# A masked prefix sum read at one row: the two blind blocks as the first pair of the buffer cycle, and two remainders a round

## The chip, the cores and the metric

The kernel runs on one core of a Trainium2 chip. The metric is the time of one execution on the device in microseconds. The profile is of one such execution; its times count from the start of its span. "Landing" is the moment at which a transfer's last part has signalled. TensorE does the matmuls, VectorE the small vector work, ScalarE (ACT) and SyncE (SP) issue the loads, and GpSimd (POOL) writes a few constants.

## The reference

```python
B, S, D = 8, 8192, 512            # x [B, S, D] f32, lengths [B] int64, w [D, D] f32
mask = (pos < lengths[:, None, None]).astype(np.float32)
cs = np.cumsum(x * mask, axis=1)
midpoints = (lengths // 2).clip(0)
mid_features = cs[b_idx, midpoints, :]
out = np.matmul(mid_features[:, None, :], w).squeeze(1)
```

Only one row of the prefix sum is wanted for each batch, so out[b] is the sum of the first min(lengths[b] // 2 + 1, lengths[b]) rows of x[b], times w. How many rows that is, the kernel learns when it has read `lengths`.

## The kernel before

**Blocks and rests.** The rows of a batch are read in blocks of 512 rows (1 MB, `P` = 128 partitions x `G` = 4 rows). What is left over, under 512 rows, is the batch's rest. It is read in pieces of 256, 128, 64, 32 or 16 rows into one of three buffers `rem`. Everything is summed by TensorE into one accumulator `s_ps`: the weights (`cur`, `cur_rem`) are 0 or 1 and say to which of the eight batches a block belongs or, for a rest, which partitions count. A block is four matmuls (one for each of its four rows a partition) that run in four column groups of the array.

**The blind blocks.** The first block of batch 0 and that of batch 1 are loaded before `lengths` is known (L187 to L190), into a tile of their own, `first`. Their weights `cur_first` are 1 where the batch has such a block. They are multiplied ahead of the loop (L549 to L552).

**The cycle.** All other whole blocks, but for the last one of the last batch, go in pairs through a buffer `xt` of `NS` = 3 places, `PER` = 6 blocks a round. VectorE works out from `lengths` how many there are (`addr[1]`), at which row each begins (`addr`), and the weights of each (`since`). Four engines run over the same rounds with semaphores between them:

- SP (L216 to L247): `load(k)` waits until place k is free (`s_free[k]`), issues one 2 MB load, or two of 1 MB where the two blocks do not touch, or a single block at the end, then loads the next two addresses.
- TensorE (L555 to L574): in place k it first issues `BUSY[k]` idle matmuls (`keep_busy`), which keep the array busy while it waits, then waits for `s_full[k]`, multiplies the pair, and then the rest that this round has for place k.
- VectorE (L471 to L494): when TensorE is done with place k it writes the weights of that place's next pair into `cur[:, k]`, which frees the place for SP; in the same way `cur_rem[:, k]` for rests, which frees a rest buffer for ACT.
- ACT (L275 to L324): issues the loads of the rests, three a round, so eight rests take three rounds.

A test ahead of each place (`pairs`, L153) skips it where no block is left for it, on each of these engines. A rest is multiplied in a round as long as `some`, which falls by three a round, says so.

**The end.** The last whole block of the last batch has its own tile `last`, loaded in four parts on SP's queue behind all others (L253 to L255). TensorE adds its first two quarters to `s_ps`, then signals VectorE (`tell`, L530), which copies `s_ps` to `s_sb` in two halves. TensorE folds and turns these into `t_ps`, VectorE moves them to `t_sb`, and 16 matmuls with w give the output, which goes out in two halves.

**VectorE's list.** VectorE begins with 59 steps in a fixed order, and others wait on their count: `DVE_ADDR` (15) lets SP start, `DVE_FIRST` (32) lets TensorE multiply the blind blocks, `DVE_MASK` (49) lets it enter the loop, `DVE_ALL` (59) ends the list.

Of the kernel before, what the change touches and what calls it, by code (L numbers as in the profile page):

```python
# [12 lines left out]
ds = bass.ds  # L13
# [4 lines left out]
def kernel(  # L18
# [34 lines left out]
    PER = 2 * NS  # L53
    ROUNDS = -(-(B * S // 2 // BLK - BLIND - 1) // PER)
    ITEMS = BLIND + ROUNDS * PER
    KC = D // P
# [8 lines left out]
    WT = G * B  # L65
    RR = -(-B // NS)
    xf = x.rearrange("b s d -> (b s) d")
# [14 lines left out]

    first = sb("first", [P, BLIND, G, D])
    xt = sb("xt", [P, NS, 2, G, D])
    last = sb("last", [P, G, D])
    rem = sb("rem", [P, NS, G, D])
    wt = sb("wt", [P, KC, D])
    lens1 = sb("lens1", [1, 2 * NS * RR], I32)
    len_f = sb("len_f", [1, B])
# [26 lines left out]
    row_last = sb("row_last", [1, 1], I32)  # L116
    cur_first = sb("cur_first", [P, BLIND, B])
    cur = sb("cur", [P, NS, 2, B])
# [7 lines left out]
    thr = sb("thr", [P, G], I32)  # L126
    table = sb("table", [P, max(B * (WT + 1), NS * RR * WT)])
    cur_rem = sb("cur_rem", [P, NS, WT])
    fold_i = sb("fold_i", [P, B], I32)
# [12 lines left out]
    s_done, s_free, s_full = [[sem(f"{n}{k}") for k in range(NS)] for n in ("done", "free", "full")]  # L142
    s_rdone, s_rfree, s_rem = [[sem(f"{n}{q}") for q in range(NS)] for n in ("rdone", "rfree", "rem")]
    s_last = [sem(f"last{h}") for h in range(len(ENDS))]
    s_first = [sem(f"first{b}") for b in range(BLIND)]
    s_w, s_len1, s_out = sem("w"), sem("len1"), sem("out")
# [33 lines left out]

    nc.sync.dma_start(out=lens1[:, :2 * B], in_=lens_words).then_inc(s_len1, 16)

# [4 lines left out]
    for b in range(BLIND):  # L187
        nc.sync.dma_start(
            out=first[:, b], in_=xf[b * S:b * S + BLK].rearrange("(p g) d -> p g d", g=G)
        ).then_inc(s_first[b], 16)  # L190

# [17 lines left out]
    def _(sp):  # L209
# [5 lines left out]

        def load(k):  # L216
            take(sp, s_free[k], 1)

            def block(h, n=1):

                to = xt[:, k].rearrange("p h g d -> p (h g) d")[:, h * G:(h + n) * G]
                sp.dma_start(
                    out=to, in_=xf[ds(sp.snap(at[h]), n * BLK)].rearrange("(p g) d -> p g d", g=n * G)
                ).then_inc(s_full[k], 16)

            sp.reg_alu(apart, at[1], at[0], ALU.subtract)
            with sp.If_cmp(left, 2 * k + 2, "IS_GE"):
                with sp.If_cmp(apart, BLK, "IS_EQ"):
                    block(0, 2)
                    sp.sem_inc(s_full[k], 16)  # L230
                with sp.Else():
                    block(0)
                    block(1)
            with sp.Else():
                block(0)
                sp.sem_inc(s_full[k], 16)
            if k == NS - 1:
                sp.wait_ge(s_dve, DVE_ALL)
            sp.load(at, addr[:, ds(sp.snap(off, min_val=BLIND + 2, max_val=ITEMS - 2), 2)])
            sp.reg_alu(off, off, 2, ALU.add)  # L240
            sp.reg_alu(off, off, ITEMS - 2, ALU.min)
# [19 lines left out]
    def _(act):  # L261
        hint = act.mark_branch_hint_location()
        alu = act.reg_alu
        base, at, t = [act.alloc_register(f"act_{n}") for n in ("base", "at", "t")]
        words = [act.alloc_register(f"act_n{i}") for i in range(2 * NS)]
        pair, top = act.alloc_register("act_pair"), 2 * NS * (RR - 1)
        some = act.alloc_register("act_some")
        act.reg_mov(base, 0)
        act.reg_mov(pair, 0)
        act.reg_mov(some, B)  # L270
        act.memzero(lens1[:, 2 * B:])  # L271
        for q in range(NS):
            act.memzero(rem[:, q]).then_inc(s_rfree[q], 1)  # L273
        act.wait_ge(s_len1, 16)
        with act.Fori(0, RR):  # L275
            act.load(words, lens1[:, ds(act.snap(pair, min_val=0, max_val=top), 2 * NS)])
            def rest(q):
# [37 lines left out]
                alu(base, base, S, ALU.add)  # L315
            for q in range(NS):
                if q < B - NS * (RR - 1):
                    rest(q)
                else:
                    with act.If_cmp(some, q + 1, "IS_GE"):  # L320
                        rest(q)
            less(act, some, NS)
            alu(pair, pair, 2 * NS, ALU.add)
            alu(pair, pair, top, ALU.min)  # L324
# [10 lines left out]
    def _(pool):  # L335
# [8 lines left out]
        pool.iota(fold_i[:], pattern=[[-1, B]], base=128, channel_multiplier=1).then_inc(s_pool, 1)  # L344
        for k in range(NS):
            pool.sem_inc(s_free[k], 1)
# [4 lines left out]
    def _(dve):  # L351
# [20 lines left out]
        dve.wait_ge(s_len1, 16)  # L372
        step(dve.tensor_copy, out=len_f[:], in_=lens1[:, :2 * B:2])
        assert done == DVE_N, done
# [7 lines left out]
        def addresses(a, b):  # L382
# [7 lines left out]
        dve.wait_ge(s_pool, 1)  # L390
        step(dve.tensor_tensor, out=above[:], in0=shape(lens1[:, :2 * B:2].unsqueeze(2), 1, B, K), in1=steps[:],
             op=ALU.is_ge)
# [13 lines left out]
        step(dve.memset, since[:, B:], 0.0)  # L406
        step(dve.memset, cur_first[:], 0.0)
        step(dve.memset, bits[:], 256)
# [11 lines left out]

        step(dve.tensor_copy, out=cur_first[:].rearrange("p k b -> p (k b)")[:, ::B + 1], in_=has[:, :BLIND])
        step(dve.tensor_copy, out=addr[:, :1], in_=has[:1, B - 1:])
# [4 lines left out]
        sinces(begin, 0, ITEMS)  # L427
        step(dve.tensor_tensor, out=cur[:].rearrange("p k h b -> p b (k h)"), in0=since[:, :B, BLIND:BLIND + PER],
             in1=since[:, 1:, BLIND:BLIND + PER], op=ALU.subtract)

# [12 lines left out]
        step(dve.tensor_tensor, out=thr[:, 2:], in0=thr_i[:], in1=shape(m4[:], P, 2), op=ALU.mult)  # L443
        tab = table[:, :B * (WT + 1)].rearrange("p (b q) -> p b q", b=B)
        step(dve.tensor_tensor, out=cap[:], in0=shape(cnt[:].unsqueeze(2), P, B, G),
             in1=shape(bits[:].unsqueeze(1), P, B, G), op=ALU.bitwise_and)
        step(dve.tensor_tensor, out=tab[:, :, 0:G * B:B], in0=cap[:],
             in1=shape(thr[:].unsqueeze(1), P, B, G), op=ALU.is_gt)
        rests = table[:, :NS * RR * WT].rearrange("p (r q w) -> p r q w", q=NS, w=WT)
        step(dve.tensor_copy, out=cur_rem[:], in_=rests[:, 0])  # L450
# [16 lines left out]
        dve.load([left], addr[:, 1:2])  # L467
        dve.reg_mov(at, BLIND + PER)
        dve.reg_mov(of, 1)
        dve.reg_mov(some, B - NS)  # L470
        with dve.Fori(1, rounds_of(dve, left, RR)):  # L471
            less(dve, left, PER)

            def weights(k):
                take(dve, s_done[k], 1)
                here = ds(dve.snap(at, min_val=BLIND + PER, max_val=ITEMS - PER) + 2 * k, 2)
                dve.tensor_tensor(  # L477
# [4 lines left out]
            for k in range(NS):  # L482
                pairs(dve, left, weights, k, k + 1)
                with dve.If_cmp(some, k + 1, "IS_GE"):
                    take(dve, s_rdone[k], 1)
                    dve.tensor_copy(  # L486
                        out=cur_rem[:, k],
                        in_=rests[:, ds(dve.snap(of, min_val=1, max_val=RR - 1), 1), k].rearrange("p o w -> p (o w)"),
                    ).then_inc(s_rfree[k], 1)
            less(dve, some, NS)  # L490
            dve.reg_alu(at, at, PER, ALU.add)
# [18 lines left out]
    def _(pe):  # L510
# [34 lines left out]
        pe.wait_ge(s_dve, DVE_FIRST)  # L545
        pe.load([has_last, left], addr[:, :2])
        pe.reg_mov(some, B)
        rounds = rounds_of(pe, left, RR)
        for b in range(BLIND):  # L549
            pe.wait_ge(s_first[b], 16)  # L550
            for j in range(G):
                add(j, cur_first[:, b], first[:, b, j])  # L552
        BUSY = [3, 1, 0]
        pe.wait_ge(s_dve, DVE_MASK)
        with pe.Fori(0, rounds):  # L555
            def add_pair(k):
                keep_busy(BUSY[k])
                take(pe, s_full[k], 32)
                with pe.If_cmp(left, 2 * k + 2, "IS_GE"):
                    for j in range(G):  # L560
                        add(j, cur[:, k, 1], xt[:, k, 1, j])
                for j in range(G):
                    mm = add(j, cur[:, k, 0], xt[:, k, 0, j])
                mm.then_inc(s_done[k], 1)

            for k in range(NS):
                pairs(pe, left, add_pair, k, k + 1)
                with pe.If_cmp(some, k + 1, "IS_GE"):
                    take(pe, s_rem[k], 16 * (len(PARTS) + 1))
                    for j in range(G):  # L570
                        mm = add(j, cur_rem[:, k, j * B:(j + 1) * B], rem[:, k, j])
                    mm.then_inc(s_rdone[k], 1)
            less(pe, left, PER)
            less(pe, some, NS)  # L574

# [61 lines left out]
```

## Time and profile before

| | us |
|---|---|
| median of 14 runs | 84.35 |
| lowest, highest | 84.15, 86.21 |
| the profiled execution | 84.46 |
| its span | 82.4 |
| TensorE busy, of it idle matmuls | 57.4, 16.1 |
| VectorE, ACT, POOL busy | 15.0, 7.4, 1.3 |
| HBM read, mean rate | 31.23 MB, 379 GB/s |

The page lists busy times by engine, then the span in 40 slices of 2.06 us, with the busy share in tenths and the rate of the transfers. Then come the chain of waits that ended last, groups of instructions by line and tile (busy time, mean length in ns, what the engine waited for before), and the issues of transfers with the median time from issue to landing. Busy times of matmuls are those of their modelled ends; four matmuls in four column groups overlap.

### The profile page before, as it was taken

What the parts mean: (1) busy time and instruction counts of PE and PEld (TensorE: products, weight loads), DVE (VectorE), ACT (ScalarE), POOL (GpSimd) and SP (SyncE); (2) the same over time, 40 slices, a digit from 0 to 9 for tenths busy, and PEclk for the clock granted to TensorE, in tenths of its full rate; (3) what the DMA queues carried; (4) which work ended last, traced back from release to release, by engine and by line L of the source; (5) the groups of instructions that cost most, each with busy time, mean ns of one, the idle gap of its engine ahead of it and who ended that gap; (6) DMA issues with size and microseconds to landing.
All of it is one profiled execution on the core that took longest, in us unless ns stands there. A gap on an engine that the chain in (4) does not pass through costs nothing. (4 is left out here: it accounts for less than half of the span.)

```text
span 82.4 us, 1513 instructions
## 1 busy us (share of the span) xinstructions
PE 57.4 (70%) x389; PEld 15.1 (18%) x389; DVE 15.0 (18%) x79; ACT 7.4 (9%) x8; POOL 1.3 (2%) x14
## 2 busy tenths in 40 slices
PE   2800699589089599992198099999957989196820
PEld 2300005021012024220011021412201422011510
DVE  2758887101000100010000000000000000000620
ACT  0999300000000000000000000000000000000020
POOL 5000000000000000000000000000000000000000
PEclk9999999999965999999759957999999999999997
DMA  1999999999999999999999999999999999999000
GB/s 18 368 382 430 458 434 428 428 430 390 462 430 402 410 430 402 414 422 398 461 407 406 449 447 411 434 421 438 422 414 454 430 414 438 402 396 377 19 1 6
DMA packets 3826, 31.25 MB, mean 379 GB/s; under 512 B 562, under 2 KB 834, under 8 KB 1618
## 3 DMA queue, kind: packets, MB, share of 16 engines
q1 hardware_dynamic: 2754, 27.27, 78.8%
q10 hardware_dynamic: 1072, 3.97, 12.4%
HBM read 31.23 MB, written 0.02 MB: 379 GB/s over the span
## 5 line engine op out<-in xcount | busy, mean ns | idle before, releaser
L513 PE MATMUL s_ps<-xt,cur 128*8 128x512 f32 x184 | 26.5, 699 | 14.6 <-PEq L151 14.6
L528 PE MATMUL idle_ps<-idle 128*128 128x512 f32 x32 | 16.1, 625 | 0.0
L513 PEld LDWEIGHTS s_ps<-xt,cur 128*8 128x8 f32 x184 | 4.3, 94 | 33.8 <-issue 33.8
L477 DVE TENSOR_TENSOR cur<-since 128x16 f32 x9 | 1.7, 187 | 44.5 <-DVEq L151 44.5
L513 PE MATMUL s_ps<-rem,cur_rem 128*8 128x512 f32 x64 | 8.5, 598 | 0.0
L528 PEld LDWEIGHTS idle_ps<-idle 128*128 128x128 f32 x32 | 5.6, 197 | 11.6 <-issue 11.6
L513 PE MATMUL s_ps<-first,cur_first 128*8 128x512 f32 x16 | 3.6, 1041 | 5.1 <-DVE since L360 5.1
L329 ACT COPY o_sb<-o_ps 8x128 f32<-8x128 f32 x2 | 0.5, 258 | 69.9 <-PE o_ps L600 69.9
L273 ACT ACTIVATE rem<-rem 128x2048 uint32<-128x2048 uint32 x3 | 5.5, 1893 | 0.0
L513 PEld LDWEIGHTS s_ps<-rem,cur_rem 128*8 128x8 f32 x64 | 2.0, 101 | 6.8 <-issue 6.8
L539 PE MATMUL s_ps<-zero 1*128 1x512 f32 x2 | 2.1, 1136 | 1.6 <-DVE zero L360 1.6
L360 DVE COPY s_sb<-s_ps 128x256 f32<-128x256 f32 x2 | 0.8, 424 | 11.6 <-PE idle_ps L532 11.5
L513 PEld LDWEIGHTS s_ps<-first,cur_first 128*8 128x8 f32 x16 | 0.2, 90 | 6.7 <-issue 5.1
L486 DVE COPY cur_rem<-table 128x32 f32 x5 | 0.9, 181 | 3.1 <-DVEq L151 3.1
L271 ACT ACT_TABLE_LOAD x1 | 1.3, 1283 | 1.9 <-issue 1.9
L600 PE MATMUL o_ps<-wt,t_sb 128*8 128x128 f32 x32 | 1.1, 273 | 0.1
L360 DVE TENSOR_TENSOR part_a<-since,step_a 1x42 f32<-1x42 f32 (+1 forms) x2 | 1.1, 560 | 0.1
L521 PE MATMUL t_ps<-last,e_last 128*8 128x64 f32 x32 | 1.0, 220 | 0.1
L360 DVE TENSOR_TENSOR since<-item,begin 1x42 f32<-1x42 int32 (+1 forms) x2 | 0.8, 423 | 0.1
L600 PEld LDWEIGHTS o_ps<-wt,t_sb 128*8 128x8 f32 x32 | 0.8, 89 | 0.3 <-issue 0.3
L542 PEld LDWEIGHTS n_ps<-len_f,ones 1*128 1x128 f32 x2 | 0.7, 332 | 1.0 <-DVE len_f L360 0.5
L539 PEld LDWEIGHTS s_ps<-zero 1*128 1x128 f32 x2 | 0.5, 306 | 1.6 <-DVE zero L360 1.6
(70 smaller groups left out, 14.3 us busy)
## 6 DMA issues: line engine op xcount, KB each, us to landing
xt<-in_x_dram SPq DMA_DIRECT2D x10, 2048.0 KB, 12.5
xt<-in_x_dram SPq DMA_DIRECT2D x3, 1024.0 KB, 9.4
first<-in_x_dram SPq DMA_DIRECT2D x2, 1024.0 KB, 7.7
rem<-in_x_dram ACTq DMA_DIRECT2D x3, 512.0 KB, 8.8
wt<-in_w_dram ACTq DMA_DIRECT2D x2, 512.0 KB, 5.5
rem<-in_x_dram ACTq DMA_DIRECT2D x3, 256.0 KB, 7.8
last<-in_x_dram SPq DMA_DIRECT2D x1, 512.0 KB, 7.6
rem<-in_x_dram ACTq DMA_DIRECT2D x3, 128.0 KB, 8.0
```

Source lines behind the costliest of these rows:

```text
L271: act.memzero(lens1[:, 2 * B:])
L273: act.memzero(rem[:, q]).then_inc(s_rfree[q], 1)
L329: copy = act.copy(out=o_sb[1][:, j * P:(j + 1) * P], in_=o_ps[64 + 32 * j:64 + 32 * j + B, :P])
L360: do(*args, **kw).then_inc(s_dve, 1)
L477: dve.tensor_tensor(out=cur[:, k], in0=since[:, :B, here].rearrange("p b h -> p h b"), in1=since[:, 1:, here].rearrange("p b h -> p h b"), ...
L486: dve.tensor_copy(out=cur_rem[:, k], in_=rests[:, ds(dve.snap(of, min_val=1, max_val=RR - 1), 1), k].rearrange("p o w -> p (o w)"),).then_ ...
L513: return pe.matmul(s_ps[32 * j:32 * j + B, columns], lhsT=weights, rhs=rows[:, columns], start=False, stop=False, skip_group_check=True, t ...
L521: mm = pe.matmul(t_ps[h][32 * j:32 * j + B, :P // 2], lhsT=weights, rhs=row[:, at:at + P // 2], start=False, stop=False, skip_group_check= ...
L528: pe.matmul(idle_ps[:], lhsT=idle[:], rhs=idle[:, :1].to_broadcast((P, D)), start=True, stop=True)
L539: pe.matmul(s_ps[:], lhsT=zero[:], rhs=zero[:, :1].to_broadcast((1, D)), start=True, stop=False, skip_group_check=True)
L542: pe.matmul(n_ps[:, :B], lhsT=ones[:], rhs=len_f[:], start=True, stop=True).then_inc(s_pe, 1)
L600: mm = pe.matmul(o_ps[32 * j:32 * j + B, :P], lhsT=t_sb[:, kc, :B], rhs=wt[:, kc, j * P:(j + 1) * P], start=(kc == 0), stop=(kc == KC - 1) ...
```

## The change

The blind blocks are loaded into place 0 of `xt` instead of `first`, and are the cycle's first pair; the tile `first`, its weights and its semaphores go. The count of blocks in the cycle is now two higher on TensorE and VectorE. SP's first load therefore goes to place 1, then 2, then 0, and place 0 is not declared free at the start. TensorE has no work left ahead of the loop, and it enters the loop when `DVE_MASK` is reached. Rests use `NR` = 2 buffers, two a round, so eight take four rounds; only places 0 and 1 have a rest. `BUSY` becomes 3, 1, 1, and in place 0 the idle matmuls are issued only where the place gets two blocks. ACT zeroes two rest buffers instead of three, and a small zeroing of padding behind `lengths` goes.

```diff
-    ROUNDS = -(-(B * S // 2 // BLK - BLIND - 1) // PER)
-    ITEMS = BLIND + ROUNDS * PER
+    ROUNDS = -(-(B * S // 2 // BLK - 1) // PER)
+    ITEMS = ROUNDS * PER
...
+    NR = 2
-    RR = -(-B // NS)
+    RR = -(-B // NR)
...
-    first = sb("first", [P, BLIND, G, D])
-    rem = sb("rem", [P, NS, G, D])
+    rem = sb("rem", [P, NR, G, D])
...
     for b in range(BLIND):
         nc.sync.dma_start(
-            out=first[:, b], in_=xf[b * S:b * S + BLK].rearrange("(p g) d -> p g d", g=G)
-        ).then_inc(s_first[b], 16)
+            out=xt[:, 0, b], in_=xf[b * S:b * S + BLK].rearrange("(p g) d -> p g d", g=G)
+        ).then_inc(s_full[0], 16)
...
-        def load(k):
+        def load(i):
+            k = (i + 1) % NS
             take(sp, s_free[k], 1)
...
-            with sp.If_cmp(left, 2 * k + 2, "IS_GE"):
+            with sp.If_cmp(left, 2 * i + 2, "IS_GE"):
...
-        act.memzero(lens1[:, 2 * B:])
-        for q in range(NS):
+        for q in range(NR):
             act.memzero(rem[:, q]).then_inc(s_rfree[q], 1)
...
-        for k in range(NS):
+        for k in range(1, NS):
             pool.sem_inc(s_free[k], 1)
...
-        step(dve.tensor_copy, out=cur_first[:].rearrange("p k b -> p (k b)")[:, ::B + 1], in_=has[:, :BLIND])
+        step(dve.tensor_copy, out=cur[:, 0].rearrange("p h b -> p (h b)")[:, ::B + 1], in_=has[:, :BLIND])
...
         dve.load([left], addr[:, 1:2])
+        dve.reg_alu(left, left, BLIND, ALU.add)
...
             for k in range(NS):
                 pairs(dve, left, weights, k, k + 1)
-                with dve.If_cmp(some, k + 1, "IS_GE"):
-                    take(dve, s_rdone[k], 1)
+                if k < NR:
+                    with dve.If_cmp(some, k + 1, "IS_GE"):
+                        take(dve, s_rdone[k], 1)
...
         pe.load([has_last, left], addr[:, :2])
+        pe.reg_alu(left, left, BLIND, ALU.add)
...
-        for b in range(BLIND):
-            pe.wait_ge(s_first[b], 16)
-            for j in range(G):
-                add(j, cur_first[:, b], first[:, b, j])
-        BUSY = [3, 1, 0]
+        BUSY = [3, 1, 1]
         pe.wait_ge(s_dve, DVE_MASK)
         with pe.Fori(0, rounds):
             def add_pair(k):
-                keep_busy(BUSY[k])
-                take(pe, s_full[k], 32)
-                with pe.If_cmp(left, 2 * k + 2, "IS_GE"):
+                def second():
                     for j in range(G):
                         add(j, cur[:, k, 1], xt[:, k, 1, j])
+
+                if k:
+                    keep_busy(BUSY[k])
+                    take(pe, s_full[k], 32)
+                    with pe.If_cmp(left, 2 * k + 2, "IS_GE"):
+                        second()
+                else:
+                    with pe.If_cmp(left, 2, "IS_GE"):
+                        keep_busy(BUSY[k])
+                        take(pe, s_full[k], 32)
+                        second()
+                    with pe.Else():
+                        take(pe, s_full[k], 32)
                 for j in range(G):
                     mm = add(j, cur[:, k, 0], xt[:, k, 0, j])
                 mm.then_inc(s_done[k], 1)
 
             for k in range(NS):
                 pairs(pe, left, add_pair, k, k + 1)
-                with pe.If_cmp(some, k + 1, "IS_GE"):
-                    take(pe, s_rem[k], 16 * (len(PARTS) + 1))
...
-                    mm.then_inc(s_rdone[k], 1)
+                if k < NR:
+                    with pe.If_cmp(some, k + 1, "IS_GE"):
+                        take(pe, s_rem[k], 16 * (len(PARTS) + 1))
...
+                        mm.then_inc(s_rdone[k], 1)
             less(pe, left, PER)
-            less(pe, some, NS)
+            less(pe, some, NR)
```

More of the change, by code (lines that the diff above doesn't have):

```diff
@@ L81, in sem @@
         return tc.alloc_semaphore(name)
-    first = sb("first", [P, BLIND, G, D])
     xt = sb("xt", [P, NS, 2, G, D])
     last = sb("last", [P, G, D])
-    rem = sb("rem", [P, NS, G, D])
+    rem = sb("rem", [P, NR, G, D])
     wt = sb("wt", [P, KC, D])
-    lens1 = sb("lens1", [1, 2 * NS * RR], I32)
+    lens1 = sb("lens1", [1, 2 * B], I32)
     len_f = sb("len_f", [1, B])
@@ L116 @@
     row_last = sb("row_last", [1, 1], I32)
-    cur_first = sb("cur_first", [P, BLIND, B])
     cur = sb("cur", [P, NS, 2, B])
@@ L126 @@
     thr = sb("thr", [P, G], I32)
-    table = sb("table", [P, max(B * (WT + 1), NS * RR * WT)])
-    cur_rem = sb("cur_rem", [P, NS, WT])
+    table = sb("table", [P, B * (WT + 1)])
+    cur_rem = sb("cur_rem", [P, NR, WT])
     fold_i = sb("fold_i", [P, B], I32)
@@ L142 @@
     s_done, s_free, s_full = [[sem(f"{n}{k}") for k in range(NS)] for n in ("done", "free", "full")]
-    s_rdone, s_rfree, s_rem = [[sem(f"{n}{q}") for q in range(NS)] for n in ("rdone", "rfree", "rem")]
+    s_rdone, s_rfree, s_rem = [[sem(f"{n}{q}") for q in range(NR)] for n in ("rdone", "rfree", "rem")]
     s_last = [sem(f"last{h}") for h in range(len(ENDS))]
-    s_first = [sem(f"first{b}") for b in range(BLIND)]
     s_w, s_len1, s_out = sem("w"), sem("len1"), sem("out")
@@ L178 @@
     PE_ALL, PE_SUM, PE_OUT = 2, 3, 5
-    nc.sync.dma_start(out=lens1[:, :2 * B], in_=lens_words).then_inc(s_len1, 16)
+    nc.sync.dma_start(out=lens1[:], in_=lens_words).then_inc(s_len1, 16)
     for h in range(2):
@@ L236, in load @@
                 sp.sem_inc(s_full[k], 16)
-            if k == NS - 1:
+            if i == NS - 1:
                 sp.wait_ge(s_dve, DVE_ALL)
@@ L264, in _ @@
         base, at, t = [act.alloc_register(f"act_{n}") for n in ("base", "at", "t")]
-        words = [act.alloc_register(f"act_n{i}") for i in range(2 * NS)]
-        pair, top = act.alloc_register("act_pair"), 2 * NS * (RR - 1)
-        some = act.alloc_register("act_some")
+        words = [act.alloc_register(f"act_n{i}") for i in range(2 * NR)]
+        pair, top = act.alloc_register("act_pair"), 2 * NR * (RR - 1)
         act.reg_mov(base, 0)
         act.reg_mov(pair, 0)
-        act.reg_mov(some, B)
-        act.memzero(lens1[:, 2 * B:])
-        for q in range(NS):
+        for q in range(NR):
             act.memzero(rem[:, q]).then_inc(s_rfree[q], 1)
@@ L275, in _ @@
         with act.Fori(0, RR):
-            act.load(words, lens1[:, ds(act.snap(pair, min_val=0, max_val=top), 2 * NS)])
+            act.load(words, lens1[:, ds(act.snap(pair, min_val=0, max_val=top), 2 * NR)])
             def rest(q):
@@ L315, in rest @@
                 alu(base, base, S, ALU.add)
[L316 to L323, printed above, removed]
+            for q in range(NR):
+                rest(q)
+            alu(pair, pair, 2 * NR, ALU.add)
             alu(pair, pair, top, ALU.min)
@@ L372, in _ @@
         dve.wait_ge(s_len1, 16)
-        step(dve.tensor_copy, out=len_f[:], in_=lens1[:, :2 * B:2])
+        step(dve.tensor_copy, out=len_f[:], in_=lens1[:, ::2])
         assert done == DVE_N, done
@@ L390, in _ @@
         dve.wait_ge(s_pool, 1)
-        step(dve.tensor_tensor, out=above[:], in0=shape(lens1[:, :2 * B:2].unsqueeze(2), 1, B, K), in1=steps[:],
+        step(dve.tensor_tensor, out=above[:], in0=shape(lens1[:, ::2].unsqueeze(2), 1, B, K), in1=steps[:],
              op=ALU.is_ge)
@@ L406, in _ @@
         step(dve.memset, since[:, B:], 0.0)
-        step(dve.memset, cur_first[:], 0.0)
+        step(dve.memset, cur[:], 0.0)
         step(dve.memset, bits[:], 256)
@@ L427, in _ @@
         sinces(begin, 0, ITEMS)
-        step(dve.tensor_tensor, out=cur[:].rearrange("p k h b -> p b (k h)"), in0=since[:, :B, BLIND:BLIND + PER],
-             in1=since[:, 1:, BLIND:BLIND + PER], op=ALU.subtract)
+        step(dve.tensor_tensor, out=cur[:].rearrange("p k h b -> p b (k h)")[:, :, BLIND:],
+             in0=since[:, :B, BLIND:PER], in1=since[:, 1:, BLIND:PER], op=ALU.subtract)
         step(dve.tensor_scalar, out=m4[:], in0=pid[:], scalar1=3, scalar2=None, op0=ALU.bitwise_and)
@@ L443, in _ @@
         step(dve.tensor_tensor, out=thr[:, 2:], in0=thr_i[:], in1=shape(m4[:], P, 2), op=ALU.mult)
-        tab = table[:, :B * (WT + 1)].rearrange("p (b q) -> p b q", b=B)
+        tab = table[:].rearrange("p (b q) -> p b q", b=B)
         step(dve.tensor_tensor, out=cap[:], in0=shape(cnt[:].unsqueeze(2), P, B, G),
@@ L448, in _ @@
              in1=shape(thr[:].unsqueeze(1), P, B, G), op=ALU.is_gt)
-        rests = table[:, :NS * RR * WT].rearrange("p (r q w) -> p r q w", q=NS, w=WT)
+        rests = table[:, :B * WT].rearrange("p (r q w) -> p r q w", q=NR, w=WT)
         step(dve.tensor_copy, out=cur_rem[:], in_=rests[:, 0])
@@ L467, in _ @@
         dve.load([left], addr[:, 1:2])
-        dve.reg_mov(at, BLIND + PER)
+        dve.reg_alu(left, left, BLIND, ALU.add)
+        dve.reg_mov(at, PER)
         dve.reg_mov(of, 1)
-        dve.reg_mov(some, B - NS)
+        dve.reg_mov(some, B - NR)
         with dve.Fori(1, rounds_of(dve, left, RR)):
@@ L475, in weights @@
                 take(dve, s_done[k], 1)
-                here = ds(dve.snap(at, min_val=BLIND + PER, max_val=ITEMS - PER) + 2 * k, 2)
+                here = ds(dve.snap(at, min_val=PER, max_val=ITEMS - PER) + 2 * k, 2)
                 dve.tensor_tensor(
@@ L483, in _ @@
                 pairs(dve, left, weights, k, k + 1)
-                with dve.If_cmp(some, k + 1, "IS_GE"):
-                    take(dve, s_rdone[k], 1)
[L486 to L490, printed above, removed]
+                if k < NR:
+                    with dve.If_cmp(some, k + 1, "IS_GE"):
+                        take(dve, s_rdone[k], 1)
+                        dve.tensor_copy(
+                            out=cur_rem[:, k],
+                            in_=rests[:, ds(dve.snap(of, min_val=1, max_val=RR - 1), 1), k].rearrange("p o w -> p (o w)"),
+                        ).then_inc(s_rfree[k], 1)
+            less(dve, some, NR)
             dve.reg_alu(at, at, PER, ALU.add)
@@ L567, in _ @@
                 pairs(pe, left, add_pair, k, k + 1)
-                with pe.If_cmp(some, k + 1, "IS_GE"):
-                    take(pe, s_rem[k], 16 * (len(PARTS) + 1))
-                    for j in range(G):
-                        mm = add(j, cur_rem[:, k, j * B:(j + 1) * B], rem[:, k, j])
-                    mm.then_inc(s_rdone[k], 1)
+                if k < NR:
+                    with pe.If_cmp(some, k + 1, "IS_GE"):
+                        take(pe, s_rem[k], 16 * (len(PARTS) + 1))
+                        for j in range(G):
+                            mm = add(j, cur_rem[:, k, j * B:(j + 1) * B], rem[:, k, j])
+                        mm.then_inc(s_rdone[k], 1)
             less(pe, left, PER)
-            less(pe, some, NS)
+            less(pe, some, NR)
         with pe.If_cmp(has_last, 1, "IS_GE"):
```

## The prediction

> **What bounds the kernel now.** I read the page's 40 slices first.
>
> ```profile
> DMA  1999999999999999999999999999999999999000
> GB/s 18 368 382 430 458 434 428 428 430 390 462 430 402 410 430 402 414 422 398 461 407 406 449 447 411 434 421 438 422 414 454 430 414 438 402 396 377 19 1 6
> ```
>
> From slice 1 to slice 36 (2 to 76 us) the transfer engines are never below nine tenths, at about 420 GB/s, and no byte moves afterwards except the output. TensorE is busy for 57.4 us of 82.4, 16.1 of these on idle matmuls. So there are only two ways to change the time: a gap in the stream of transfers, or the path behind its last bytes. A faster or slower pair in the middle counts only if it leaves the queue without work.
>
> The page's issue table gives the amount of work:
>
> ```profile
> xt<-in_x_dram SPq DMA_DIRECT2D x10, 2048.0 KB, 12.5
> xt<-in_x_dram SPq DMA_DIRECT2D x3, 1024.0 KB, 9.4
> ```
>
> Ten whole pairs, one pair in two halves and one single block: 23 blocks. I call the blind pair P0, the eleven pairs P1 to P11, and the single block P12.
>
> **Part 1, moving the blind pair.** Its two loads keep their place in SP's queue (issued at 1.3 and 1.7 us); only their target and semaphore change. Before, three pair loads followed at 6.27, 8.47 and 10.55 us, all into empty places. Now P1 and P2 go out at the first two of these times, and P3's place still holds P0. SP stops there until P0 has been multiplied and VectorE has freed the place; nothing but later loads queue behind that wait, and `last` and the output are far away. From P4 on nothing moves: before and after, P(n) needs the place of P(n-3).
>
> How long does the queue live without P3? It holds w 1024, P0 2048, P1 and P2 4096 and the first two rests 128+256+32 KB: 7584 KB, or 7.77 MB. The third rest (512 KB, issued at 13.35 us before) is now behind P0 too. A table of stretches of the trace says what had been moved by 20.59 us:
>
> ```profile
> 0.00:20.59 20.59, 12.70 (x52) 3.56 (x52) 10.86 (x61) 6.90 (x6) 1.27 (x14) 1.00 0.91 376
> ```
>
> 376 GB/s (last column) x 20.59 us = 7.74 MB, so the queue runs dry at about 20.7 us.
>
> When does P3's load come? These timeline rows (start, length, engine, operation) carry it:
>
> ```profile
> 12.47 3.06 PE L528 MATMUL idle_ps<-idle 128*128 128x512 f32 x6
> 16.77 1.90 PE L513 MATMUL s_ps<-xt,cur 128*8 128x512 f32 x16 [1.24 <-PEq L151]
> 18.99 0.19 DVE L477 TENSOR_TENSOR cur<-since 128x16 f32 x1 [4.32 <-DVEq L151]
> 19.76 0.34 SPq L222 DMA_DIRECT2D xt<-in_x_dram  x1
> 23.79 0.19 PEld L513 LDWEIGHTS s_ps<-xt,cur 128*8 128x8 f32 x4 [0.62 <-issue]
> 24.64 0.19 PEld L513 LDWEIGHTS s_ps<-xt,cur 128*8 128x8 f32 x4 [0.67 <-issue]
> ```
>
> A pair is four groups of four matmuls that run side by side. A group takes 0.43 us at the full clock (four groups from 16.77 to 18.48), 0.855 us at half clock (24.64 less 23.79). From the end of a pair to the next load's issue it is 19.76 less 18.67, 1.09 us, through VectorE and SP. From issue to first byte it is 0.83 us on an idle queue (output issued at 79.44; no byte before 80.27).
>
> VectorE's masks are ready at 11.63 us (its `cur_rem` copy ends there; the few changed sizes in its list save under 0.1 us). TensorE then passes the loop's start and two compares, some 0.3 us, and begins its idle matmuls at 11.95: six matmuls, each as long as a group. Before, the blind blocks' matmuls ran from 8.94 at 1041 ns each, half clock, and warmed the array, so that the idle matmuls behind them soon ran at 0.43. Now the idle matmuls come first and are cold themselves. Here a rule and a row differ in outcome. The row: in this run the array came to full clock at 12.92, 4.0 us after work began. The Trainium skill ("TensorE: Matmul & The Clock Gate", Part 1) says that the window of about 3.4 us runs freely, so that the switch depends on where in it the work begins. If the windows stay where this run has them (12.92 + 3.41 = 16.33), 5.1 of the ten units (six idle, four groups) are cold and 4.9 warm: 16.33 + 2.1 + 0.2 for the drain = 18.6, and P3 is issued at 19.7, as before; its first byte comes at 20.55, and there is no gap. By the rule, the switch lies anywhere from 15.36 to 18.77: P0 ends at 18.1 to 19.8, the first byte comes at 20.05 to 21.75, the gap is 0 to 1.05 us, on average 0.3. I take 0.2 us, between the row and the rule's mean, and keep 0 and 1.05.
>
> Afterwards there is slack. P0's rest and one idle matmul pair put P1 at about 20.1 and its reload at 23; P3 alone feeds the queue until 26, the third rest until 27. P2 is done at 25.3, reload at 26.5. Each later reload comes some 5 us or more before the queue is empty.
>
> **Part 2, two rests a round.** Eight rests now take four rounds. Each is 0.86 us of matmul, beside transfers. The last comes behind P10, which before landed at about 67 us, 5 us ahead of P11: hidden; without that cover it would cost 0.86. ACT loses one zeroing of 1.89 us and the small one of 0.20, and VectorE a copy to a third place, both off the path. The rests' bytes are the same, so 0. A rest reloaded behind P0 may land a microsecond after TensorE asks for it; P4 is waited for then anyway.
>
> **Part 3, idle matmuls.** The third place gets one (two instructions, 0.86 us) ahead of P2, P5, P8, P11. Even the largest bill at full clock, three idle matmuls and a pair, is 2.6 + 1.9 = 4.5 us against 5.0 us for a pair's 2.1 MB. 0. At half clock this cover is gone, but the queue's backlog of one pair or more then hides it.
>
> **Part 4, the end.** Here I expect the main cost. 2 + 23 = 25 blocks is four rounds and one block: P12 now opens a fifth round alone. Before, it was the third place of the fourth, next to the loop's exit. The rows of TensorE's end:
>
> ```profile
> 74.82 1.04 PE L513 MATMUL s_ps<-xt,cur 128*8 128x512 f32 x8 [0.75 <-PEq L151]
> 75.68 0.12 PEld L513 LDWEIGHTS s_ps<-last,e_last 128*8 128x8 f32 x8 [0.75 <-DMA last<-in_x_dram]
> ```
>
> and of its branches in that stretch, asked for line by line:
>
> ```profile
> L559 PEldq COMPARE_BRANCH  x1: 223/223/223, 74.5 to 74.5; - x1
> L568 PEldq COMPARE_BRANCH  x1: 228/228/228, 74.8 to 74.8; - x1
> L171 PEldq FUSED_REGOPS  x1: 83/83/83, 75.1 to 75.1; - x1
> L576 PEldq COMPARE_BRANCH  x1: 79/79/79, 75.4 to 75.4; - x1
> ```
>
> A compare that jumps takes 0.22 to 0.23 us and 0.285 to the next instruction; one that falls through, 0.07 to 0.08. Before, behind P12 there was one jump (L568), registers, and two compares; the sequencer stood at the wait for `last` at 75.5, and `last` landed at 75.64: a slack of 0.15 us. After, P12's own test precedes its wait, so its matmuls can start at 74.55 instead of 74.82. But four blocks must then be jumped over: the first place's rest, the second pair, its rest, the third pair. 74.56 + 4 x 0.285 + 0.14 (registers) + 0.13 + 0.1 (two compares) = 76.07 us, 0.4 later than 75.68. Behind that wait stand `last`'s matmuls, the signal, both copies of `s_sb`, the fold, the product: the chain of waits runs through all of it, so the 0.4 reaches the end.
>
> The Trainium skill ("Advanced Engine Details and Errata", Control Flow Timing) gives a compare-and-branch about 108 ns. By that the four cost 0.43 and the sequencer arrives at 75.4: nothing is lost. The trace's own jumps, on this engine and in this stretch, are the nearer row: I take 0.4. The ends: 0 if jumps overlap, 0.7 if the closing branch of the new else-arm, which no row shows, costs another 0.28.
>
> **Sum.** 0.2 + 0.4 = 0.6 us. The profiled execution took 84.46 with a span of 82.4; it would be 85.06 and 83.0. The median of the runs is 0.11 below it: 84.35 + 0.6 = 84.95.
>
> **Rivals.** *Jumps hidden* (other side): the new jumps cost under 0.19 us each, or `last` lands 0.4 us later behind P12 than now; then TensorE still waits for `last`, and with no gap in front the time is 84.35, with 0.2 of gap 84.55. For it: the skill's figure, and that other sequencer work runs ahead of matmuls. Against: L568, 0.285 to its successor in this very place. *Cold start*: the clock switches in the last part of its window, so the queue stands empty for 1.05 us, plus 0.4 behind: 85.8. For it: SP's load depends on a chain with no other cover. Against: this run's own windows. *Better transfers*: eight of the slices 3 to 35 move less than 410 GB/s, several of them beside rests; rests two at a time might lift these. 0.5% of 74 us would be 0.37: 84.6 with the 0.6 lost, 84.0 with neither loss. Against: bytes and pieces are the same. *Not as described*: P12 opens a fifth round alone only because 23 blocks are read; with 22 or 24 the tests of part 4 would fall elsewhere. The issue table excludes this.
>
> **Numbers.** Forecast 0.5, jumps hidden 0.2, cold start 0.15, better transfers 0.1, an unlooked-for cost of the shifted code 0.05. The range leaves out the far ends of the last two: 84.2 to 85.8. About 0.3% (0.25 us) can be told from no change here. Slower: forecast, cold start, shifted code, less some of the forecast's low end, 0.68. Same: 0.22. Faster: 0.10.
>
> **What would show it.** Right: the third SP load of `xt` at 19.2 to 20.9 us with at most a dip in slice 10 of GB/s; `last`'s weight loads held by issue, about 0.4 us behind its landing, no longer by the transfer; four jumps before it. Wrong: `last`'s matmuls still released by its transfer, or a hole of over 1 us near 21 us, or loads from P4 on with the queue empty.

## The result, and the profile after

| us | before | changed |
|---|---|---|
| median (lowest to highest) | 84.47 (84.09 to 86.61), 47 runs | 86.8 (85.63 to 88.12), 10 runs |
| ratio, 95% interval | | 1.0192 (1.0159 to 1.0225) |
| the profiled execution, its span | 84.46, 82.4 | 86.35, 84.5 |
| landing of `last`'s first part | 75.64 | 77.48 |
| first matmul on `last` | 75.68 | 77.91 |

The change makes the kernel slower, by 1.6 to 2.3% by the interval and 2.3 us by the medians; 84.95 was predicted, with 85.8 as the upper end. The ratio leaves out every run that is over 1.5% above the fastest of its kernel, four of the changed kernel's ten; they are probably part of its own wider spread of 2.5 us, and so the medians lie further apart than the ratio.

The two profiled executions differ by 2.2 us of span (84.54 and 82.36 before rounding). Of this, 1.84 is there when `last` lands, and 0.39 more when it is multiplied. From there on the two kernels take the same steps at the same lengths. The page's rates of the changed kernel show where the first part begins:

```profile
DMA  1999999996999999999999999999999999997000
GB/s 23 372 384 434 461 422 403 450 438 287 240 415 434 438 450 392 399 426 454 440 378 443 423 444 419 430 407 425 458 390 440 419 450 411 407 395 274 1 8 8
```

Slices 9 and 10 (19.0 to 23.2 us) move 287 and 240 GB/s, where they moved 390 and 462 before. (390 + 462 - 287 - 240) x 2.1 / 420 = 1.6 us of transfers. No other stretch is lower than before by anything like that. The timeline of the changed kernel up to that point (start, length, engine, line):

```profile
11.92 5.48 PE L521 MATMUL idle_ps<-idle 128*128 128x512 f32 x6 [8.04 <-DVE cur_rem L351]
...
17.32 1.92 PE L506 MATMUL s_ps<-xt,cur 128*8 128x512 f32 x16
19.57 0.19 DVE L469 TENSOR_TENSOR cur<-since 128x16 f32 x1 [5.05 <-DVEq L149]
...
20.33 0.34 SPq L221 DMA_DIRECT2D xt<-in_x_dram  x1
```

The six idle matmuls ran at half clock throughout: 5.4 us from the first to the blind pair's first matmul, and the array came to full speed only with that pair (the granted clock's record has the switch at 17.41 us). So P3's load was issued at 20.33 us, within the predicted 19.2 to 20.9. What happened to the queue is seen in one stretch of 2.5 us, first before, then changed (columns: stretch, its length, busy time and count for PE, PEld, DVE, ACT, POOL, granted clock, share of time in which the transfer engines held a packet, GB/s):

```profile
20.50:23.00 2.50, 0.09 (x1) 0.00 (x0) 0.00 (x0) 0.00 (x0) 0.00 (x0) 1.00 1.01 426
```

```profile
20.50:23.00 2.50, 2.50 (x22) 0.56 (x24) 0.07 (x1) 0.00 (x0) 0.00 (x0) 1.00 0.69 157
```

The last two columns must be read together. The engines held packets for 0.69 of the stretch but moved only 157/426 = 0.37 of the bytes. So they were empty for 0.31 x 2.5 = 0.8 us, and for another 0.32 x 2.5 = 0.8 us they held packets that did not get on. These columns count a packet where it begins, so the split is rough, but the packet records say the same: a 16 KB packet takes 611 ns in the steady stream. The first that each engine took after the empty stretch needed 830 to 2150 ns (14 of the 16 are on record), and four of the second ones needed 950 to 1330.

The end of the changed kernel, in the chain of waits and then in two rows of TensorE's branches:

```profile
70.28 7.20 DMA last<-in_x_dram
77.48 0.43 issue
77.91 0.62 PE s_ps L506 x8
```

```profile
L570 PEldq COMPARE_BRANCH  x2: 208/211/214, 76.4 to 77.0; - x2
```

```profile
L154 PEldq COMPARE_BRANCH  x2: 208/213/218, 76.7 to 77.2; - x2
```

"Issue" is time in which the engine waited for nothing that the profile shows. `last` landed at 77.48; the sequencer was still on its way, through the four jumps from 76.37 to 77.50 and the registers and compares behind them.

### The profile page after: what moved, and what is told of

It is laid out like the page before. It is cut to its first block, busy times and chain, and to the rows that moved or that the text cites. A ratio compares the mean times of both kernels' runs of the same rounds, so it can differ in the third digit from the quotient of the medians.

```text
span 84.5 us, 1544 instructions
## 1 busy us (share of the span) xinstructions
PE 61.1 (72%) x397; PEld 16.9 (20%) x397; DVE 15.3 (18%) x81; ACT 5.5 (7%) x6; POOL 1.3 (1%) x14
## 5 line engine op out<-in xcount | busy, mean ns | idle before, releaser
L506 PE MATMUL s_ps<-xt,cur 128*8 128x512 f32 x200 | 27.1, 662 | 9.4 <-PEq L149 9.3
L521 PE MATMUL idle_ps<-idle 128*128 128x512 f32 x40 | 23.1, 697 | 8.0 <-DVE cur_rem L351 8.0
L521 PEld LDWEIGHTS idle_ps<-idle 128*128 128x128 f32 x40 | 7.5, 212 | 24.1 <-issue 24.1
L269 ACT ACTIVATE rem<-rem 128x2048 uint32<-128x2048 uint32 x2 | 3.7, 1901 | 0.0
L506 PE MATMUL s_ps<-last,e_last 128*8 128x256 f32 x8 | 0.6, 380 | 0.5 <-DMA last<-in_x_dram 0.5
L514 PE MATMUL t_ps<-s_sb,fold 128*8 128x64 f32 x16 | 0.6, 221 | 0.2 <-DVE s_sb L351 0.2
```

What stands on the lines that cost most here:

```text
L506: return pe.matmul(s_ps[32 * j:32 * j + B, columns], lhsT=weights, rhs=rows[:, columns], start=False, stop=False, skip_group_check=True, t ...
L514: mm = pe.matmul(t_ps[h][32 * j:32 * j + B, :P // 2], lhsT=weights, rhs=row[:, at:at + P // 2], start=False, stop=False, skip_group_check= ...
L521: pe.matmul(idle_ps[:], lhsT=idle[:], rhs=idle[:, :1].to_broadcast((P, D)), start=True, stop=True)
```

## The experiments

Twelve kernels ran. Names that begin with b_ are the kernel before with an edit; the others are the changed kernel with an edit. The kernel before had 84.38 us in the first set (idle0, rests3, exit, idle0_exit), 84.39 in the second (idle2, idle4, b_rests2, b_jumps3), and 84.48 in the third.

Two readings per engine, averaged over 16, are worked out from the packet records from 20 us until the stream is steady again: time without a packet ("empty"), and time by which packets of 8 KB and more took longer than the steady 309 or 611 ns ("slow"). "Landing" is by how much `last`'s first part landed later than 75.64.

| us | P3's load issued | empty | slow | landing | median (range) |
|---|---|---|---|---|---|
| idle0 | 17.11 | 0 | 0.03 | 0 | 84.66 (84.5 to 85.1) |
| rests3 | 19.27 | 0.05 | 0.19 | 0.57 | 85.7 (85.26 to 86.31) |
| idle2 | 19.31 | 0.22 | 0.56 | 1.47 | 85.95 (84.68 to 86.71) |
| changed | 20.33 | 0.78 | 0.81 | 1.84 | 86.8 (85.63 to 88.12) |
| exit | 20.31 | 0.66 | 0.83 | 1.41 | 85.83 (85.55 to 86.17) |
| idle4 | 20.85 | 1.47 | 0.72 | 2.09 | 86.28 (85.90 to 86.69) |
| split | 20.14 | 0.88 | 0.24 | 1.32 | 85.87 (85.21 to 87.27) |
| b_late16 | 22.67 | 2.01 | 0.74 | 2.53 | 86.84 (86.64 to 86.99) |
| b_late24 | 26.54 | 5.62 | 0.87 | 6.40 | 90.63 (90.53 to 90.74) |

**idle0: no idle matmuls ahead of the blind pair.**

```diff
                     with pe.If_cmp(left, 2, "IS_GE"):
-                        keep_busy(BUSY[k])
                         take(pe, s_full[k], 32)
...
                 mm.then_inc(s_done[k], 1)
+                if k == NS - 1:
+                    with pe.If_cmp(left, PER + 2, "IS_GE"):
+                        keep_busy(BUSY[0])
```

> The changed kernel, but the three idle matmuls of the first place are issued at the end of the third place's work instead, so that none stands ahead of the blind pair. Theory (dry queue and slow restart): the blind pair is done by about 15.6 us and P3's load goes out at about 16.5, long before the queue is dry at 20.7; no dip in the rate near 21 us, the front loss of 1.8 us is gone, what stays is 0.4 for the jumps: 84.9 us, and the spread of the runs shrinks to that of the kernel before. Rival (the new order of loads and rests moves its bytes more slowly as such): no gap, but still about 86.3 us.

84.66 us, 1.0040 (1.0027 to 1.0054) of the kernel before. The same stretch in its trace:

```profile
20.50:23.00 2.50, 2.50 (x18) 0.66 (x18) 0.18 (x1) 0.00 (x0) 0.00 (x0) 1.00 1.01 429
```

Full share and full rate: the whole front loss is gone, `last` lands at 75.62, and the spread of 13 runs is 0.6 us. The rival, that the new order moves bytes more slowly as such, falls. The end is still late, 0.44 us behind the landing:

```profile
76.06 0.62 PE L506 MATMUL s_ps<-last,e_last 128*8 128x256 f32 x8 [0.54 <-DMA last<-in_x_dram]
```

**exit: one jump at the end.** `more` is a register, set ahead of the first place.

```diff
-            for k in range(NS):
-                pairs(pe, left, add_pair, k, k + 1)
+            def rest(k):
                 if k < NR:
...
+            pe.reg_alu(more, left, 2, ALU.subtract)
+            pe.reg_alu(more, more, some, ALU.max)
+            pairs(pe, left, add_pair, 0, 1)
+            with pe.If_cmp(more, 1, "IS_GE"):
+                rest(0)
+                for k in range(1, NS):
+                    pairs(pe, left, add_pair, k, k + 1)
+                    rest(k)
```

> The changed kernel, where one test behind the first place's pair skips all that is left of a round with no more pairs and no more rests: one jump at the end instead of four. Theory (jumps): last's matmuls start at its landing again, about 0.4 us less than the changed kernel, the dip near 21 us unchanged: about 86.0 us. Rival (the end is set by the transfers alone): no change against the changed kernel.

85.83 us, ratio to before 1.0187 (1.0147 to 1.0228). Its front is as in the changed kernel, and `last`, landed at 77.05, is multiplied at once:

```profile
77.09 0.62 PE L506 MATMUL s_ps<-last,e_last 128*8 128x256 f32 x8 [0.15 <-DMA last<-in_x_dram]
```

The spread of the front makes the times a weak witness here: the medians lie 0.97 us apart, but by the ratios (1.0187 against 1.0192) the two kernels can't be told apart. The 0.04 us between landing and matmul, instead of 0.43, is the reading.

**idle0_exit: both edits.**

> Both of these edits: no idle matmuls ahead of the blind pair, and one jump at the end. Theory (the two losses are all there is): the time of the kernel before, 84.45 us within 0.2. Rival (something else of the change costs too): 84.9 us or more.

84.3 us (84.04 to 84.46, 12 runs), 0.9967 (0.9941 to 0.9993) of the kernel before, and 0.36 us less than idle0, which differs from it by the jumps alone. `last` landed at 75.70 and is multiplied 0.05 us later:

```profile
75.75 0.62 PE L506 MATMUL s_ps<-last,e_last 128*8 128x256 f32 x8 [0.15 <-DMA last<-in_x_dram]
```

With both losses undone, no other cost of the change is left to see; if there is a gain, it is at the limit of what these runs can tell.

**rests3: three rests a round, the rest of the change kept.**

```diff
-    NR = 2
+    NR = 3
```

> The changed kernel with three rests a round and three rest buffers as before; the blind pair stays the first pair of the cycle. Theory (dry queue and slow restart): the third rest, 512 KB, is in the queue again from 13.4 us and feeds it 1.25 us longer, to about 21.9, and P3's first byte comes at about 21.2: no gap or a small one, 85.1 us (0.4 for the jumps of the changed kernel and 0.27 for a fifth jump). Rival (bytes move more slowly in the new order): 86.3 us or more.

85.7 us, 0.6 more than expected. In this trace the array came to full clock at 15.15 us, not 17.41, so P3's load went out 1.06 us earlier than in the changed kernel's trace, and the two can't be compared directly. idle2 below, with P3's load at 19.31, is the nearer partner: 0.22 us empty there, 0.05 here, where the third rest's packets run on to 22.24 us. So the third rest does feed the queue.

Even so four of P3's first packets took 950 to 1430 ns, with work in the queue until then. Why was not shown. `last`'s fifteenth engine landed 0.13 later than before, the last one 0.57. At the end the five jumps held `last`'s weight loads 0.70 us behind the landing; its matmuls came 0.84 behind, since the array, at half clock until 76.59, was still busy with P12. The rival, 86.3 or more, does not hold for the median.

**b_rests2: two rests a round, alone.** The kernel before, with `NR` = 2 wherever rests are counted.

> The kernel before with one part of the change alone: two rests a round, the blind blocks in their own tile as before. Theory (the loss comes from P3's load alone): the queue is never dry, no jump is added, 84.4 us within 0.2. Rival (two rests a round cost something themselves): 84.8 us or more.

84.38 us (20 runs), ratio 0.9997 (0.9978 to 1.0016). Two rests a round cost nothing by themselves. With rests3 this says where they matter: the third rest's 512 KB would have fed the queue where P3's load was late.

**idle2 and idle4: how many idle matmuls it takes.** As idle0, with two or four of them once ahead of the loop.

> As idle0, but with two idle matmuls once, ahead of the loop, so that the blind pair starts one idle matmul sooner than in the changed kernel. Theory (dry queue and slow restart, a threshold): P3's load goes out about 0.9 to 1.5 us sooner than the changed kernel's 20.3, its first byte comes before the queue is dry, and the time is that of idle0: 84.7 us. Rival (each idle matmul ahead of the blind pair costs its own length): two thirds of the way from idle0's 84.66 to the changed kernel, 85.8 us.

> As idle2, with four. Theory (threshold): the queue is dry already with three; a fourth idle matmul lengthens the gap by its own length, 0.43 us at full clock to 0.86 at half clock: 86.7 to 87.3 us. Rival (proportional from the first): 86.9 us; idle2 tells these apart.

85.95 us (84.68 to 86.71) for two, 86.28 us (85.90 to 86.69) for four: neither stated time came. Both edits also let the idle matmuls begin 0.36 us sooner (11.56 us instead of 11.92), since they no longer stand inside the loop.

Two are not free: single runs lie at 84.68, at no loss, and up to 86.71. In the profiled one the clock switched at 17.45, as late as in the changed kernel's trace, and P3's load was issued at 19.31. Its bytes came just as the queue ran out:

```profile
20.50:23.00 2.50, 2.50 (x25) 0.68 (x18) 0.19 (x1) 0.00 (x0) 0.00 (x0) 1.00 0.96 328
```

The share is 0.96, so hardly an engine was empty (0.22 us), and yet the rate is 328 GB/s: the first packets of P3 were as slow here as behind a long gap (0.56 us slow), and the last engine landed 1.47 us late. So in this trace the slow start needed no gap; it also hits a load that comes at the last moment.

Four cost no more than the changed kernel's three by the medians (86.28), but with a spread of 2.5 us, and four runs, these decide nothing. In the trace the clock switched 0.44 us earlier than in the changed kernel's, P3's load went out 0.52 us later, the queue was empty 0.69 us longer, and `last` landed 0.25 later. So a cost that grows with every idle matmul is not ruled out. The runs fit a threshold that is a band rather than a line, with two idle matmuls in it; they do not prove it, as only one execution of each kernel has a trace.

**b_late16 and b_late24: only P3's load is late.** TensorE's order and its jumps are those of the kernel before. (b_late24 has 24 in place of 16.)

```diff
+    spare = sb("spare", [P, 16, 512])
...
-        for k in range(NS):
+        for k in range(NS - 1):
             pool.sem_inc(s_free[k], 1)
...
+        pool.wait_ge(s_dve, DVE_ALL)
+        for i in range(16):
+            held = pool.memset(spare[:, i], 0.0)
+        held.then_inc(s_free[NS - 1], 1)
```

> The kernel before, in which GpSimd declares the third place free only after 16 memsets that follow the end of VectorE's list (14.7 us), so that the third pair's load goes out later, as in the changed kernel, but with TensorE's order, the clock and the jumps of the kernel before. Here the queue also holds the third rest and lasts to about 21.9 us. Theory (dry queue and slow restart): no cost if the load goes out before about 21.0 us; later, the gap itself plus about 1 us for slow packets and uneven engines behind it. Rival (gap alone): the gap and no more, packets at their usual 611 ns.

> As b_late16, with 24 memsets: the load goes out later still. Theory (dry queue and slow restart): longer by the gap plus the same 1 us or so as in any dry case, so that two dry cases differ by their gaps alone. Rival (gap alone): the gap and no more.

b_late16's SP row, and the stretch around its gap:

```profile
22.67 0.34 SPq L223 DMA_DIRECT2D xt<-in_x_dram  x1
```

```profile
21.50:25.50 4.00, 2.41 (x19) 0.59 (x23) 0.64 (x1) 0.00 (x0) 0.61 (x2) 0.83 0.56 160
```

160/426 = 0.38 of the bytes at a share of 0.56: again about 0.7 us of packets that do not get on, without the changed kernel's order. One side effect: VectorE's copy of rest weights, which ran beside the memsets, took 2.75 us instead of 0.18, and a rest's load went out at 24.49 us instead of 22.33, so it too was missing in the gap. b_late24 does not have this (22.33), and shows the same:

```profile
21.50:29.50 8.00, 4.04 (x24) 0.72 (x24) 0.37 (x2) 0.00 (x0) 4.47 (x10) 0.79 0.31 82
```

82/426 = 0.19 of the bytes at a share of 0.31: 0.9 us. b_late24 lies 3.8 us above b_late16 by the medians, and 3.6 us more are empty; their slow parts are 0.74 and 0.87. So a dry queue costs its empty time, plus 0.7 to 0.9 us of slow packets that do not depend on its length. At the end of the kernel 0.5 (b_late16) to 0.8 us (b_late24) of landing are left beyond the empty time. "The gap alone" falls.

**split: P3, P6 and P9 in halves.** SP issues two loads of 8 KB a partition for the first place instead of one of 16 KB.

> The changed kernel, with the pairs of the first place (P3, P6, P9) always loaded in two halves of 8 KB a partition instead of one of 16 KB. The empty stretch is the same. If the slow packets of the restart come from all engines walking in step through large packets, smaller ones let them drift apart sooner, and about 0.5 us of the 0.8 us of slow packets goes: 85.8 us. Rival (the restart is slow whatever the packets): as the changed kernel, 86.3 us.

85.87 us (85.21 to 87.27). The slow part falls from 0.81 to 0.24 us. The stretch from 20.5 us in its trace:

```profile
20.50:23.00 2.50, 2.50 (x22) 0.56 (x24) 0.09 (x1) 0.00 (x0) 0.00 (x0) 1.00 0.59 210
```

A lower share than the changed kernel's 0.69 and yet a higher rate: the packets get on. But part of the loss has only changed its name. In the changed kernel the first packets began 0.96 to 1.3 us after the issue; here four engines began 1.03 to 1.08 us after it, the other twelve only 1.66 to 2.03. So the empty part is 0.88, although P3's load was issued 0.19 us earlier. Empty and slow together are 1.12 us, against 1.59; with the 0.19 taken off, some 0.3 us is left that the smaller packets can have saved, in one trace each. By the runs the two kernels can't be told apart (ratio to before 1.0114, 1.0043 to 1.0185). Why a load starts slowly was not shown.

**b_jumps3 and b_jumps3s: three more jumps at the end.**

```diff
+        for _ in range(3):
+            with pe.If_cmp(some, 1, "IS_GE"):
+                keep_busy(4)
```

> The kernel before with three more jumps (tests on a register that is then 0) between the loop and the adding of last, nothing else. Theory (jumps stand on the path behind the transfers): 3 x 0.28 less the slack of 0.15 us: 0.6 to 0.7 us more, 85.0 to 85.1 us, and last's matmuls that much behind its landing. Rival (the sequencer runs ahead, jumps are hidden): 84.4 us.

> b_jumps3 again, with one idle matmul in each of the three bodies that are jumped over instead of four, so that the program is shorter. In b_jumps3 the jumps delayed last's matmuls by 0.67 us as expected, but one of the 16 transfer engines also ran 1.3 us behind from a 16 KB instruction fetch at 32.7 us on. Theory (the longer program caused that fetch, the jumps cost 0.6 to 0.7): without the fetch 85.0 to 85.1 us. Rival (the jumps cost it all): 86.0 us again.

86.09 and 86.27 us: far over 85.1, and the second did not mend it. Two things overlap. In b_jumps3 `last`'s first part landed at 76.99 and its matmul came at 77.66, 0.67 behind; in b_jumps3s 0.64. That is the jumps, as expected. But the landing itself is 1.35 us late, and this is one engine alone: the fifteenth of the 16 had landed at 75.64, as before. The page of b_jumps3 has a row that the page before has not:

```profile
q8 instruction: 1, 0.02, 0.1%
```

The packet records date it: a 16 KB instruction fetch at 32.7 us that took 1.06 us (31.8 us and 1.07 in b_jumps3s, where the program is hardly shorter). From the load then under way on, the last of the 16 landing signals comes 1.3 to 1.8 us behind the fifteenth in every load of `xt`, to the end; in the kernel before it is at most 0.11. What makes the program fetch there is not shown. So these two runs price the jumps by their rows, not by their medians; by medians, idle0 against idle0_exit is the clean pair: 0.36 us.

## Why the prediction was wrong

It said slower, by 0.6 us; it is 2.3 by the medians. Point by point:

- **What bounds the kernel**: held. Only the stream of transfers and the path behind it counted; idle0_exit, which mends these two places, has the old time.
- **Two rests a round (0)**: held by itself (b_rests2).
- **The third place's idle matmul (0)**: held; it is also in idle0_exit.
- **The end (0.4)**: held. Four jumps, 0.27 to 0.32 us from each to the next instruction; `last`'s matmul came 0.43 behind its landing, 0.39 more than before. The trace's own jumps were the nearer row than the 108 ns of the Trainium skill ("Advanced Engine Details and Errata", Control Flow Timing), which would have made it nothing. The rival *jumps hidden* falls, and the worry about the else-arm's closing branch (another 0.28) was empty: from the wait to P12's matmuls it took 0.11 us, and the first of the four jumps followed at once.
- **When the queue runs dry (20.7 us)**: held. The engines' last packets before the gap ended from 20.6 to 21.05.
- **When P3's load is issued**: 20.33, inside the stated 19.2 to 20.9, but not at the 19.7 that this trace's clock windows gave. The switch came at 17.41, not at 16.33 as in this trace's windows, 5.5 us after the first idle matmul. In the traces of the eight kernels that have the blind pair in the cycle it came 3.1 (idle0) to 5.9 us (idle2) after TensorE's first matmul there. So the rule of the Trainium skill ("TensorE: Matmul & The Clock Gate", Part 1) that these windows run freely was the better guide, though two of the eight switched up to 0.3 us before the range worked out from it. The runs' spread of 2.5 us, against 0.6 with idle0, fits a switch that falls differently in each run.
- **The gap (0.2, at most 1.05)**: this is the step that failed; the front cost 1.84 us. With the issue at 20.33 the prediction's own formula gives 20.33 + 0.83 - 20.7 = 0.46 us, so taking the earlier switch explains only 0.26 of the miss. Three terms were mis-sized or missing. First, the issue-to-first-byte time was taken from the 8 KB output; here the first packets began 0.96 to 1.3 us after the issue, and the empty time was 0.78. Second, the sum knew only empty time. The restart at less than half rate costs 0.6 to 0.9 us more in every row from idle2 on but split, and in idle2 with hardly a gap. Third, the 16 engines did not come out of it together: the first and the last landing of `last`'s first part lay 1.16 us apart instead of 0.41. On average they landed 1.39 us later than before, the last one, which decides, 1.84. *Cold start*, the rival with 1.05 + 0.4, had the right mechanism; its 1.05 is somewhat over half of what the front cost.

The cause was thus argued rightly up to the point where the queue is empty, and then priced as if a queue came back at full speed. That it comes back slowly is shown; why it does stays open.

## What to carry to other kernels

Where transfers bound a kernel, ask of every load that gets a new wait whether the queue can empty before its first byte, and price an empty queue at its gap plus a restart, not at the gap alone. Here the restart was 0.5 to 1.1 us (landing less empty time, in the rows of changed, exit, idle4, b_late16 and b_late24). A load that comes just in time can pay for the restart too (idle2). Do not put idle matmuls ahead of work that a load waits for while the array is still cold: here six instructions took 5.4 us, where 2.6 would do at full clock, and the switch came 3.1 to 5.9 us after the first matmul, where the program does not set it. A loop's last short round should leave by one test, since each part that is jumped over costs 0.27 to 0.32 us on the path behind the last landing.

## What the runs showed of the hardware that was not expected

- After an empty stretch the first 16 KB packet of almost every engine takes 830 to 2150 ns instead of 611, and the second one of a few, whether the stretch was 0.7 or 5.6 us. In idle2 it is so with hardly an empty stretch. With 8 KB packets (split) the packets are faster, but most begin later.
- With an instruction fetch of 16 KB (1.06 us) in the middle of a stream, one of each load's 16 landing signals comes 1.3 to 1.8 us behind the others from then on, to the end (b_jumps3, b_jumps3s).
- On TensorE's sequencer, in the end stretches shown, a compare that jumps takes 0.21 to 0.23 us, one that falls through 0.07 to 0.08.
